# The first rotated queries leave from another buffer, their stores are split by head pair, and the second rope table and stores move in SP's order

## The chip, the core and the metric

The kernel runs on one core of a Trainium2 chip. Its engines are TensorE (PE; its weight loads are shown as PEld), VectorE (DVE), ScalarE (ACT), GpSimd (POOL) and SyncE (SP), which here issues every DMA transfer. Each engine works through its own list of instructions in order, and semaphores tie the lists together. The metric is the device time of one execution in microseconds, lower is better.

## What is computed

One layer on 512 tokens and 16 learned meta tokens (528 positions, width 1024): a norm, one joint projection, two attention branches of 16 heads each (MLA with a rotated part of 32 dimensions, and FoX with a forget gate), and a gated merge. Cut to what matters:

```python
u = rmsnorm(h, pre_norm_g)
(cq, ckv, k_pe_raw, z_mla, fq, fk, fv, f_logit, z_fox, gate_a, gate_b) = split(u @ w_in)
q  = (rmsnorm(cq, g) @ w_uq).reshape(L, 16, 64 + 32)      # q_nope, q_pe
kv = (rmsnorm(ckv, g) @ w_ukv).reshape(L, 16, 64 + 64)    # k_nope, v_mla
q_m = concat(q_nope, rope(q_pe, pos)); k_m = concat(k_nope, rope(k_pe_raw, pos))
o_mla = causal_attention(q_m, k_m, v_mla, scale)
cum   = cumsum(log_sigmoid(f_logit + b))
o_fox = causal_attention(fq, fk, fv, scale, cum)          # logit[t,s] += cum[t] - cum[s]
mixed = (sigmoid(gate_a) * ((o_mla * silu(z_mla)) @ w_a)
       + sigmoid(gate_b) * ((o_fox * silu(z_fox)) @ w_b)) @ w_out
out   = h + rmsnorm(mixed, post_norm_g)
```

## The kernel before

**Numbers in two halves.** Products must be nearly exact, so each operand is kept as a high half and a low half (what rounding left over), and a product is three passes: high by high, high by low, low by high. A weight tile of 128x1024 is loaded by SP (wraw, 512 KB), its high half wh is cast by ACT (L125) and its low half wl is subtracted by POOL (L100). There are three such buffers.

**Stages.** Attention runs in 16 stages, two for each of the eight head pairs: first FoX (even stages, br = 1), then MLA (odd stages, br = 0). So stage 0 is FoX on pair 0, stage 1 is MLA on pair 0, and so on. A stage has these steps:

- score products st into PSUM; DVE takes them out with the mask and the row minimum (sf, nb, L634); ACT takes the exponentials and their sums (L642)
- norm: DVE's reciprocal, then ACT and DVE write the probabilities pn as float16 halves (L669, L670), POOL the piece for the meta tokens (L656 to L661)
- eight DMA transposes by SP turn pn into pt, four blocks of queries for each of two heads. "Turning transfers" below means these.
- values: the products ov of pt and the turned values vp. These wait in the list late and run in the next stage, after its first score products.

Between these PE runs fills, which belong to later stages: projections of queries (fq, mq), keys (fk, mk), values (v), the z gates and the merge gates pg. Each such unit, when it begins, also issues the weight loads of the next three units.

**The rotated queries.** The MLA scores also need the rotated part of the queries for each head. pe_unit(g) makes it for the eight heads of half g: ppe products, DVE's products with a cos and sin table (rope_pe, 512 KB), then rest(x) for x = 0, 1 on POOL: one sum or difference (L518), a cast to the high half (L520), a subtraction for the low half (L100), and two stores to the DRAM tensor qpe_dram (L523). load_qp(pr) later loads one pair back as the tile QP. Half 0 is made before stage 0, half 1 in stages 5 and 6. For half 0 the tables and both halves lie in the room of pt, which is not in use before stage 0's turning transfers; for half 1 they lie in gT, the buffers of the branch outputs.

**What sets the order.** The schedule of PE in the attention is the order of the code. On the other engines a scheduler places instructions by readiness and priority. From the step in_order to the end of stage 0, written[0] is set, and every transfer issued by the helper dma() is then kept in the order of the code on SP's queue. SP takes its list strictly in order: a transfer whose source is not ready holds up all behind it.

**Names in the order lists.** pt_655 and pt_656 are the turned probabilities of the two heads, pn_653 and pn_654 the probabilities, vh and vp_658 / vp_659 the values before and after turning (MLA / FoX), gT_676 and gT_677 the two gT buffers, CT the forget sums of a pair. The wraw numbers of the two builds differ by a few from one point on: 904 before is 943 in the change (weights of fq for pair 1), then 977 (fk) and 993 (v) in both.

Of the kernel before, what the change touches and what calls it, by code (L numbers as in the profile page):

```python
# [49 lines left out]
def f32(ap):  # L50
    return ap.bitcast(F32)
# [3 lines left out]
def block_kernel(ctx: ExitStack, tc: tile.TileContext, x, meta_tokens, pre_norm_g, w_in, fox_forget_b,  # L55
                 mla_q_norm_g, mla_kv_norm_g, w_uq, w_ukv, w_br_mla, w_br_fox, w_out, post_norm_g,
                 rope_tok, rope_pe, out):
    nc = tc.nc
# [20 lines left out]
    c_dram = dram.tile([2, NH, L], F32, tag="cdram", name="c_dram")  # L79
    qpe_dram = dram.tile([NH, 2, 2, 16, S], F32, tag="qpedram", name="qpe_dram")  # L80
# [1 line left out]
    wp = ctx.enter_context(tc.tile_pool(name="wp", bufs=3))  # L82
    uid = [0]
    written = [False]
    behind = []

    def dma(out, src, start=None):

        ins = (start or nc.sync.dma_start)(out=out, in_=src)
        if written[0]:  # L90
            tc.keep_in_program_order(ins)

    def mm(*a, **k):
        nc.tensor.matmul(*a, **k)  # L94
# [4 lines left out]
    def split_lo(eng, lo, src, hi):  # L99
        eng.tensor_tensor(out=lo, in0=src, in1=f32(hi), op=ALU.subtract)  # L100
# [109 lines left out]
    def run(steps):  # L210
        for _, fn in steps:
            fn()
# [6 lines left out]
    CT = fx.tile([128, L], F32R, tag="CT", name="CT")  # L219
# [24 lines left out]
    def k_fox(pr):  # L244
        halves = hl_done(("k", 1, pr), L, HALF)

        def done(i, ps):
            halves(i, ps)
            if pr and i:
                for h in range(2):  # L250
                    ins = nc.sync.dma_start(out=f32(CT[64 * h : 64 * h + 2, :]), in_=c_dram[:, 2 * pr + h, :])
                    if pr == 1:

                        tc.keep_in_program_order(ins)
        return unit(f"fk{pr}", win_w(O_FK, pr), u_act, KD, ALLT, done)


# [167 lines left out]
    with ExitStack() as att:  # L425
# [15 lines left out]
        pn = [ac.tile([128, 2, n, 128], F16, tag=f"pn{g}", name=f"pn{g}") for g, n in enumerate((17, 9))]  # L441

        pts = [ac.tile([128, 9, 512], F16, tag=f"pt{h}", name=f"pt{h}") for h in range(2)]
# [13 lines left out]
        gT = [gpool.tile([128, KD, S], F32, tag=n, name=n) for n in ("gT0", "gT1")]  # L457
# [3 lines left out]
        def load_qp(pr):  # L461
            dma(f32(QP), qpe_dram[2 * pr : 2 * pr + 2].rearrange("h i x f s -> (h i x f) s"))
# [20 lines left out]
        def pe_unit(g):  # L483
            if g == 0:
                r0, tt = (p.rearrange("p a b -> p (a b)")[:, 0 : 8 * S].bitcast(F32).rearrange("p (c s) -> p c s", c=4)
                          for p in pts)
            else:
                r0, tt = gT[0][:, 4:8], gT[1][:, 4:8]
            rp = r0[:, 0:2]

            rr = [r0[:, 2:4], tt[:, 2:4]]
            if g == 0:
                nc.sync.dma_start(rp, rope_pe)
            out = []
            w = {}

            def half(xi, ws=None):
                if ws:
                    w[0] = ws
                return (lambda k: w[0][2 * xi + k][0]), (lambda k: w[0][2 * xi + k][1])  # L500

            def srcs():
                if g:
                    nc.sync.dma_start(rp, rope_pe)
                return [wuqh[:, k, 8 * g : 8 * g + 8, NOPE + 16 * x : NOPE + 16 * x + 16]
                        for x in range(2) for k in range(2)]

            for xi in range(2):
                get = (lambda: half(1)) if xi else weights(srcs, lambda ws: half(0, ws))

                def done(i, ps, xi=xi):
                    for cs in range(2):
                        nc.vector.tensor_tensor(out=tt[:, 2 * xi + cs], in0=ps, in1=rp[:, cs], op=ALU.mult)
                out += unit(f"ppe{g}{xi}", get, cq_act, 2, REAL, done)

            def rest(x):

                nc.gpsimd.tensor_tensor(out=tt[:, x], in0=tt[:, x], in1=tt[:, 3 - x], op=(ALU.subtract, ALU.add)[x])  # L518
                hi, lo = rr[x][:, 0], rr[x][:, 1]
                nc.gpsimd.tensor_copy(hi.bitcast(F32R), tt[:, x])  # L520
                split_lo(nc.gpsimd, lo.bitcast(F32R), tt[:, x], hi)
                for i in range(2):
                    dma(qpe_dram[8 * g : 8 * g + 8, i, x], rr[x][:, i])  # L523
            return out, [[(0, lambda x=x: rest(x))] for x in range(2)]

        mw = {}

# [63 lines left out]
        def attention(br, pr):  # L591
# [54 lines left out]
            def norm(g):  # L646
                def fn():
                    b0, nb_ = GRP[g][0], len(GRP[g])
                    su, ri = (sums[t][:, :, b0 : b0 + nb_] for t in ("su", "ri"))
                    nc.vector.tensor_scalar(out=su, in0=su, scalar1=1.0 / PSCALE, scalar2=None, op0=ALU.mult)  # L650
                    nc.vector.reciprocal(ri, su)  # L651

                    mt = aw.tile([128, 2, nb_, META], F32, tag=f"mt{g}", name=f"mt{nm_}{g}", bufs=1)
                    src = sfs[g][:, :, 0 : SF_STEP * nb_].rearrange("p h (b c) -> p h b c", b=nb_)[:, :, :, 0:META]
                    dst = pn[g][:, :, 0 : PN_STEP * nb_].rearrange("p h (b t) c -> p h b t c", b=nb_)[:, :, :, 0]
                    nc.gpsimd.tensor_tensor(out=mt, in0=src, in1=ri.unsqueeze(3).broadcast_to([128, 2, nb_, META]),  # L656
                                            op=ALU.mult)
                    hi, lo, hi2 = (dst[:, :, :, 32 * i : 32 * i + META] for i in range(3))
                    nc.gpsimd.tensor_copy(hi, mt)
                    nc.gpsimd.tensor_tensor(out=lo, in0=mt, in1=hi, op=ALU.subtract)  # L660
                    nc.gpsimd.tensor_copy(hi2, mt)  # L661
                    for b in GRP[g]:
                        for h in range(2):
                            sf = sf_of(h, b)[:, META:].rearrange("p (j c) -> p j c", c=128)
                            t0 = PN_STEP * (b % 3) + 1
                            hi, lo = (pn[g][:, h, t0 : t0 + 2 * b + 2].rearrange("p (j l) c -> p j l c", l=2)[:, :, i]
                                      for i in range(2))
                            rib = sums["ri"][:, h, b : b + 1]
                            nc.scalar.activation(hi, sf, AF.Copy, scale=rib)  # L669
                            nc.vector.scalar_tensor_tensor(out=lo, in0=sf, scalar=rib, in1=hi, op0=ALU.mult,  # L670
                                                           op1=ALU.subtract)
                    for b in GRP[g]:
                        for h in range(2):
                            t0 = PN_STEP * (b % 3)
                            dma(pts[h][:, 0 : 2 * b + 3, 128 * b : 128 * b + 128],
                                pn[g][:, h, t0 : t0 + 2 * b + 3].rearrange("p t c -> p (t c)"),
                                nc.sync.dma_start_transpose)
                return fn

            def values():  # L680
# [32 lines left out]
                fn.nxt = [f.load for f in fns[n + 1 : n + 4]]  # L713

        v, vts[1, 0] = v_unit(1, 0)
        pe, pe_rest = pe_unit(0)
        g = gate_unit()
        first = pe + v + [(0, in_order)] + vts.pop((1, 0)) + g[:4] + pe_rest[0] + pe_rest[1]
        begun = g[4:]
        fills = []  # L720
        for si, (br, pr) in enumerate(stages):
            last = si + 1 == len(stages)
            if not last:
                q, k, v = feed(*stages[si + 1])
            if br == 1:

                za, zb = z_unit(1, pr), z_unit(0, pr)
                fill = vts.get((br, pr), begun) + za + q + zb[:4] + k + zb[4:6] + v + zb[6:]
            elif not last:

                fill = vts[br, pr] + q + k[:KD] + v + k[KD:]
            else:
                g = gate_unit()
                fill = vts[br, pr] + g + gate_unit() + gate_unit()
            if si == 5:
                pe, pe_rest = pe_unit(1)
                fill[17:17] = pe + pe_rest[0]
            if si == 6:
                fill[17:17] = pe_rest[1]
            fills.append(fill)  # L740
        tail = gate_unit()

# [3 lines left out]
        for si, (br, pr) in enumerate(stages):  # L746
            s0, s1, n0, n1, va = attention(br, pr)

            for fn in [s0] + late + [s1]:
                fn()  # L750

            fill = fills[si]
            run(fill[:5])
            if si == 0:
                load_qp(0)
            n0()
            cut = 12 if si else 5
            run(fill[5:cut])
            n1()
            run(fill[cut:])  # L760
            written[0] = False
            if si == 1:
                behind.clear()
            late = [va]
# [146 lines left out]
```

## Time and profile before

| what | us |
|---|---|
| median of 3 runs (lowest, highest) | 628.37 (627.38, 629.66) |
| the profiled execution | 629.72 |
| its span, first to last instruction | 627.9 |
| mean granted TensorE clock, share of full | 0.994 |
| HBM read and written in the span | 55.21 MB, 4.26 MB |

The span is made up of a front part to about 69 us (norms, first projections), the attention to about 430 us, and the merge and output projection. Engine rows give a start time, a duration, the line, the operation, out<-in tiles, sizes, a count, and in brackets the idle time before it with what ended it. A row of a table by windows gives the stretch, its length, then for PE, PEld, DVE, ACT and POOL the busy time and count, the granted clock, the busy share of the 16 DMA engines and GB/s. A row of SP's queue has the time from the first issue to the end of the last; when the data has landed isn't shown there.

### The profile page before, as it was taken

What the parts mean: (1) busy time and instruction counts of PE and PEld (TensorE: products, weight loads), DVE (VectorE), ACT (ScalarE), POOL (GpSimd) and SP (SyncE); (2) the same over time, 40 slices, a digit from 0 to 9 for tenths busy, and PEclk for the clock granted to TensorE, in tenths of its full rate; (3) what the DMA queues carried; (4) which work ended last, traced back from release to release, by engine and by line L of the source; (5) the groups of instructions that cost most, each with busy time, mean ns of one, the idle gap of its engine ahead of it and who ended that gap; (6) DMA issues with size and microseconds to landing.
All of it is one profiled execution on the core that took longest, in us unless ns stands there. A gap on an engine that the chain in (4) does not pass through costs nothing.

```text
span 627.9 us, 10952 instructions
## 1 busy us (share of the span) xinstructions
PE 604.0 (96%) x3810; PEld 509.4 (81%) x3810; DVE 310.7 (49%) x899; ACT 328.9 (52%) x738; POOL 266.7 (42%) x269
## 2 busy tenths in 40 slices
PE   3999989999999999999999999999999999999996
PEld 2888877888889879789888888887888888888885
DVE  3746753567566665764674666546320122023134
ACT  5657645567665664864684666657322222232321
POOL 3225824434344652443344443541744444444620
PEclk9999997999999999999999999999999999999999
DMA  8441568868788888577579577672433333333702
GB/s 283 107 102 51 120 170 201 194 143 167 156 167 150 188 197 190 120 180 182 132 164 195 137 150 171 167 161 82 135 96 96 89 93 99 100 101 108 262 33 101
DMA packets 223808, 90.10 MB, mean 143 GB/s; under 512 B 141628, under 2 KB 216764, under 8 KB 223752
## 3 DMA queue, kind: packets, MB, share of 16 engines
q1 hardware_dynamic: 223752, 89.39, 59.7%
q8 instruction: 30, 0.49, 0.3%
q14 instruction: 26, 0.21, 0.1%
HBM read 55.21 MB, written 4.26 MB: 95 GB/s over the span
## 4 chain that ended last, share of the span: by engine, by line
PE 74%; DVE 3%; ACT 2%; issue 1%; DMA 0%; SPq 0%; DVEq 0%; ACTq 0%
PE py L94 14%; PE pg L94 13%; PE z L94 12%; PE po L94 7%; PE v L94 7%; PE fk L94 6%; PE fq L94 5%; PE st L94 4%; PE ov L94 3%; DVE sf L634 2%; PE mq L94 2%; ACT wh L125 1%; PE mk L94 1%; DVE vh L570 1%; ACT sil L583 0%
## 5 line engine op out<-in xcount | busy, mean ns | idle before, releaser
L100 POOL TENSOR_TENSOR wl<-wraw,wh 128x1024 fp32r<-128x1024 f32 (+1 forms) x90 | 208.4, 2320 | 224.6 <-ACT wh L125 222.8
L125 ACT CAST wh<-wraw 128x1024 fp32r<-128x1024 f32 (+1 forms) x90 | 89.9, 1001 | 174.8 <-issue 49.9
L642 ACT ACTIVATE sf<-sf,nb 128x144 f32<-128x144 f32 (+3 forms) x128 | 72.0, 564 | 14.9 <-DVE nb L634 14.9
L670 DVE SCALAR_TENSOR_TENSOR pn<-sf,ri,pn 128x128 f16<-128x128 f32 (+3 forms) x128 | 66.0, 554 | 13.2 <-ACT pn L669 12.3
L669 ACT ACTIVATE pn<-sf,ri 128x128 f16<-128x128 f32 (+3 forms) x128 | 61.5, 551 | 19.1 <-ACT sf L642 18.5
L794 DVE SCALAR_TENSOR_TENSOR tb<-th,py 128x512 f32<-128x512 f32 x16 | 11.0, 687 | 101.9 <-PE py L94 101.9
L94 PE MATMUL st<-hlk,hlq 64*128 64x272 f32 (+3 forms) x480 | 52.7, 318 | 1.7 <-ACT hlk L237 0.8
L94 PE MATMUL z<-uTh,wh 128*128 128x512 f32 x128 | 50.9, 398 | 0.0
L94 PE MATMUL pg<-uTh,wh 128*128 128x512 f32 x128 | 50.2, 392 | 0.0
L94 PE MATMUL z<-uTh,wl 128*128 128x512 f32 x128 | 50.0, 391 | 0.0
L94 PE MATMUL z<-uTl,wh 128*128 128x512 f32 x128 | 49.9, 390 | 0.0
L94 PE MATMUL pg<-uTl,wh 128*128 128x512 f32 x128 | 49.9, 389 | 0.0
L94 PE MATMUL pg<-uTh,wl 128*128 128x512 f32 x128 | 49.8, 389 | 0.0
L94 PE MATMUL py<-gh,wh 128*128 128x512 f32 x128 | 49.8, 389 | 0.0
L94 PE MATMUL py<-gl,wh 128*128 128x512 f32 x128 | 49.8, 389 | 0.0
L94 PE MATMUL py<-gh,wl 128*128 128x512 f32 x128 | 49.8, 389 | 0.0
L634 DVE CUSTOM_DVE_ANT_0 sf<-st,maskt 128x272 f32<-128x272 f32 (+2 forms) x128 | 48.3, 433 | 0.8 <-PE st L94 0.8
L94 PEld LDWEIGHTS st<-hlk,hlq 64*128 64x128 f32 x480 | 37.2, 189 | 11.7 <-ACT hlk L237 2.6
L656 POOL TENSOR_TENSOR mt<-sf,ri 128x96 f32<-128x96 f32 (+1 forms) x32 | 9.5, 295 | 87.3 <-DVE ri L651 66.4
L94 PE MATMUL ov<-pt,vp 128*64 128x512 f16 (+4 forms) x416 | 35.2, 318 | 4.3 <-DMA pt<-pn 4.3
L94 PEld LDWEIGHTS <-vp 128*64 128x64 f16 (+1 forms) x416 | 23.3, 113 | 18.0 <-issue 9.5
L94 PE MATMUL v<-uTh,wh 128*128 128x256 f32 (+1 forms) x128 | 36.6, 286 | 0.7 <-DVE hlq L100 0.7
(183 smaller groups left out, 1422.2 us busy)
## 6 DMA issues: line engine op xcount, KB each, us to landing
wraw<-in_w_in_dram SPq DMA_DIRECT2D x56, 512.0 KB
wraw<-in_w_br_fox_dram SPq DMA_DIRECT2D x8, 512.0 KB
wraw<-in_w_br_mla_dram SPq DMA_DIRECT2D x8, 512.0 KB
wraw<-in_w_out_dram SPq DMA_DIRECT2D x8, 512.0 KB
QP<-qpe_dram SPq DMA_DIRECT2D x8, 256.0 KB
pt<-pn SPq DMA_TRANSPOSE x128
xr<-in_x_dram SPq DMA_DIRECT2D x4, 512.0 KB
out_dram<-yo SPq DMA_DIRECT2D x8, 256.0 KB
```

What stands on the lines that cost most here:

```text
L94: nc.tensor.matmul(*a, **k)
L100: eng.tensor_tensor(out=lo, in0=src, in1=f32(hi), op=ALU.subtract)
L125: nc.scalar.copy(wh[:, :n], raw[:, :n])
L570: nc.vector.scalar_tensor_tensor(out=lo, in0=p, scalar=sc[:, 3:4], in1=hi, op0=ALU.mult, op1=ALU.subtract)
L634: nc.vector.tensor_tensor_reduce(out=sf_of(h, b)[:, c0 : c0 + w], in0=ps[h][:, o : o + w], in1=maskt[:, m0 : m0 + w], scale=-scale, scalar ...
L642: nc.scalar.activation(sf, sf, AF.Exp, bias=sums["nb"][:, h, b : b + 1], scale=-1.0, accum_out=sums["su"][:, h, b : b + 1])
L656: nc.gpsimd.tensor_tensor(out=mt, in0=src, in1=ri.unsqueeze(3).broadcast_to([128, 2, nb_, META]), op=ALU.mult)
L669: nc.scalar.activation(hi, sf, AF.Copy, scale=rib)
L670: nc.vector.scalar_tensor_tensor(out=lo, in0=sf, scalar=rib, in1=hi, op0=ALU.mult, op1=ALU.subtract)
L794: nc.vector.scalar_tensor_tensor(out=tb[br], in0=ths[i, br], scalar=1.0, in1=py, op0=ALU.add, op1=ALU.mult)
```

## The change

It has five parts:

- In pe_unit(0) the high and low halves are written to gT[0][:, 4:6] and gT[1][:, 4:6] instead of the room of pt. The table and the unrounded sums stay in pt.
- The stores of half 0 are split by head: in rest(x), two heads (pair 0) of each; the other six heads are stored in stage 1, after that stage's vp transfer.
- The table load of half 1 is kept in the order of the code.
- POOL's rest of half 1 with its stores is written after the second norm of stages 6 and 7, kept in order.
- In stage 0 the fill is cut at 4 instead of 5 steps, and both norms come right behind the load of QP; the loads of CT for pair 1 are placed after the last turning transfer of stage 0.

```diff
-            rr = [r0[:, 2:4], tt[:, 2:4]]
+            rr = [r0[:, 2:4], tt[:, 2:4]] if g else [t[:, 4:6] for t in gT]
...
                 if g:
-                    nc.sync.dma_start(rp, rope_pe)
+
+                    tc.keep_in_program_order(nc.sync.dma_start(rp, rope_pe))
...
                 split_lo(nc.gpsimd, lo.bitcast(F32R), tt[:, x], hi)
+                if g:
+                    store(x, 0, 8)
+                else:
+
+                    store(x, 0, 2)
+
+            def store(x, a, b):
                 for i in range(2):
-                    dma(qpe_dram[8 * g : 8 * g + 8, i, x], rr[x][:, i])
-            return out, [[(0, lambda x=x: rest(x))] for x in range(2)]
+                    dma(qpe_dram[8 * g + a : 8 * g + b, i, x], rr[x][16 * a : 16 * b, i])
+            return out, rest, store
...
             if si == 5:
-                pe, pe_rest = pe_unit(1)
-                fill[17:17] = pe + pe_rest[0]
-            if si == 6:
-                fill[17:17] = pe_rest[1]
+                pe, rest1, _ = pe_unit(1)
+                fill[17:17] = pe
...
-            run(fill[:5])
             if si == 0:
+
+                run(fill[:4])
                 load_qp(0)
-            n0()
-            cut = 12 if si else 5
-            run(fill[5:cut])
-            n1()
-            run(fill[cut:])
+                n0()
+                n1()
+                first_t.extend(through)
+                run(fill[4:])
+            else:
+                run(fill[:1])
+                if si == 1:
+
+                    written[0] = True
+                    for x in range(2):
+                        store0(x, 2, 8)
+                    written[0] = False
+                run(fill[1:5])
+                n0()
+                run(fill[5:12])
+                n1()
+                if 6 <= si < 8:
+
+                    written[0] = True
+                    rest1(si - 6)
+                    written[0] = False
+                run(fill[12:])
```

On PE, ACT and DVE the built lists are the same instructions in the same order. SP's list differs at three places, POOL's at one.

SP ahead of stage 0's turning transfers, before:

```order
L504 DMA gT_676<-in_rope_pe_dram 128x1024
L89 DMA_TRANSPOSE vp_659<-vh 128x9x128
L89 DMA wraw_790<-in_w_in_dram 128x8x128
L89 DMA qpe_dram<-pt_655 8x16x512 x2
L89 DMA qpe_dram<-pt_656 8x16x512 x2
L89 DMA wraw_904<-in_w_in_dram 128x8x128
L89 DMA QP<-qpe_dram 128x512
L89 DMA_TRANSPOSE pt_655<-pn_653 128x3x128
```

The same place in the change:

```order
L89 DMA_TRANSPOSE vp_659<-vh 128x9x128
L89 DMA wraw_790<-in_w_in_dram 128x8x128
L89 DMA qpe_dram<-gT_676 2x16x512 x2
L89 DMA qpe_dram<-gT_677 2x16x512 x2
L89 DMA QP<-qpe_dram 128x512
L89 DMA_TRANSPOSE pt_655<-pn_653 128x3x128
```

The second table has gone from the head (it is now in stage 3), the stores have 2 heads instead of 8, and the weight load 904 is no longer ahead of the QP load.

SP from the last turning transfer of stage 0 to the first of stage 1, before:

```order
L89 DMA_TRANSPOSE pt_656<-pn_654 128x9x128
L89 DMA wraw_977<-in_w_in_dram 128x8x128
L89 DMA wraw_993<-in_w_in_dram 128x8x128
L89 DMA_TRANSPOSE vp_658<-vh 128x9x128
L89 DMA wraw_1172<-in_w_in_dram 128x8x128
L89 DMA wraw_1231<-in_w_uq_dram 128x2x64 x2
L89 DMA wraw_1231<-in_w_ukv_dram 128x2x64 x2
L89 DMA wraw_1281<-in_w_in_dram 128x8x128
L251 DMA CT<-c_dram 2x528
L89 DMA_TRANSPOSE pt_655<-pn_653 128x3x128
```

The same place in the change:

```order
L89 DMA_TRANSPOSE pt_656<-pn_654 128x9x128
L89 DMA wraw_943<-in_w_in_dram 128x8x128
L89 DMA wraw_977<-in_w_in_dram 128x8x128
L89 DMA wraw_993<-in_w_in_dram 128x8x128
L89 DMA CT<-c_dram 2x528 x2
L89 DMA_TRANSPOSE vp_658<-vh 128x9x128
L89 DMA qpe_dram<-gT_676 6x16x512 x2
L89 DMA qpe_dram<-gT_677 6x16x512 x2
L89 DMA wraw_1176<-in_w_in_dram 128x8x128
L89 DMA wraw_1235<-in_w_uq_dram 128x2x64 x2
L89 DMA_TRANSPOSE pt_655<-pn_653 128x3x128
```

Three weight loads instead of two follow stage 0's turning transfers, and the four stores of six heads stand between the vp transfer and stage 1's turning transfers. ACT's list has the casts of all three loads (wh of 943, 977 and 993) ahead of stage 1's first exponential, as before.

SP in stage 6, before:

```order
L89 DMA wraw_2665<-in_w_in_dram 128x8x128
L89 DMA qpe_dram<-gT_676 8x16x512 x2
L89 DMA qpe_dram<-gT_677 8x16x512 x2
L89 DMA wraw_2724<-in_w_in_dram 128x8x128
L89 DMA_TRANSPOSE vp_659<-vh 128x9x128
L89 DMA wraw_2741<-in_w_in_dram 128x8x128
L89 DMA_TRANSPOSE pt_655<-pn_653 128x3x128
```

The same place in the change:

```order
L89 DMA wraw_2664<-in_w_in_dram 128x8x128
L89 DMA wraw_2723<-in_w_in_dram 128x8x128
L89 DMA_TRANSPOSE vp_659<-vh 128x9x128
L89 DMA wraw_2740<-in_w_in_dram 128x8x128
L89 DMA_TRANSPOSE pt_655<-pn_653 128x3x128
```

The four stores of half 1 have left; two now follow the last turning transfer of stage 6, two that of stage 7, where the load of QP for pair 4 stands behind them. On POOL, before stage 0, the low half of mq's weights (wl_974) now stands ahead of the casts and low halves of the rotated queries instead of behind them.

More of the change, by code (lines that the diff above doesn't have):

```diff
@@ L84, in block_kernel @@
     written = [False]
-    behind = []
+    behind, through, first_t = [], [], []
     def dma(out, src, start=None):
@@ L91, in dma @@
             tc.keep_in_program_order(ins)
+        return ins.ins
     def mm(*a, **k):
@@ L250, in done @@
                 for h in range(2):
-                    ins = nc.sync.dma_start(out=f32(CT[64 * h : 64 * h + 2, :]), in_=c_dram[:, 2 * pr + h, :])
-                    if pr == 1:
-                        tc.keep_in_program_order(ins)
+                    with tc.issue_after(first_t[0]) if pr == 1 else nullcontext():
+                        dma(f32(CT[64 * h : 64 * h + 2, :]), c_dram[:, 2 * pr + h, :])
         return unit(f"fk{pr}", win_w(O_FK, pr), u_act, KD, ALLT, done)
@@ L674, in fn @@
                             t0 = PN_STEP * (b % 3)
-                            dma(pts[h][:, 0 : 2 * b + 3, 128 * b : 128 * b + 128],
-                                pn[g][:, h, t0 : t0 + 2 * b + 3].rearrange("p t c -> p (t c)"),
-                                nc.sync.dma_start_transpose)
+                            through[:] = [dma(pts[h][:, 0 : 2 * b + 3, 128 * b : 128 * b + 128],
+                                              pn[g][:, h, t0 : t0 + 2 * b + 3].rearrange("p t c -> p (t c)"),
+                                              nc.sync.dma_start_transpose)]
                 return fn
@@ L715, in block_kernel @@
         v, vts[1, 0] = v_unit(1, 0)
-        pe, pe_rest = pe_unit(0)
+        pe, rest0, store0 = pe_unit(0)
+        pe_rest = [(0, lambda x=x: rest0(x)) for x in range(2)]
         g = gate_unit()
-        first = pe + v + [(0, in_order)] + vts.pop((1, 0)) + g[:4] + pe_rest[0] + pe_rest[1]
+        first = pe + v + [(0, in_order)] + vts.pop((1, 0)) + g[:4] + pe_rest
         begun = g[4:]
```

## The prediction

> **What bounds the kernel now.** I read the page's first part, then TensorE's own waits, then its timeline at the two places that the waits point to.
>
> ```profile
> PE 604.0 (96%) x3810; PEld 509.4 (81%) x3810; DVE 310.7 (49%) x899; ACT 328.9 (52%) x738; POOL 266.7 (42%) x269
> ```
>
> Of a span of 627.9 us, TensorE (PE) is busy for 604.0. So a change that adds no product can win only what PE waits, and what it loses to a slower clock. The waits, as total, times and longest:
>
> ```profile
> PE pt L97 <- DVE hn L337: 7.9, 2, 7.3
> PE ov L94 <- DMA pt<-pn: 4.3, 4, 2.1
> ```
>
> The 7.9 us lie at the start, where nothing changes. The second row is the one that the change is near: the value products ov wait for turned probabilities pt. Its places (start, duration, wait before it in brackets):
>
> ```profile
> 90.12 0.56 PE L94 MATMUL st<-hlk,hlq 64*128 64x144 f32 x6
> 92.13 0.35 PE L94 MATMUL st<-KPL,QP 64*128 64x400 f32 x2
> 94.59 0.45 PE L94 MATMUL ov<-pt,vp 80*64 80x512 f16 x1 [2.11 <-DMA pt<-pn]
> 95.94 3.79 PE L94 MATMUL ov<-pt,vp 80*64 80x512 f16 x25 [0.91 <-DMA pt<-pn]
> 101.93 0.50 PE L94 MATMUL fq<-uTh,wh 128*128 128x512 f32 x1
> 114.28 0.39 PE L94 MATMUL v<-uTh,wh 128*128 128x256 f32 x1 [0.68 <-DVE hlq L100]
> ...
> 182.74 0.56 PE L94 MATMUL st<-hlk,hlq 64*128 64x144 f32 x6
> 188.46 0.50 PE L94 MATMUL fq<-uTh,wh 128*128 128x512 f32 x1
> ...
> 228.10 0.56 PE L94 MATMUL st<-hlk,hlq 64*128 64x144 f32 x6
> 231.33 0.38 PE L94 MATMUL ov<-pt,vp 80*64 80x512 f16 x1 [0.86 <-DMA pt<-pn]
> 232.11 2.01 PE L94 MATMUL ov<-pt,vp 80*64 80x512 f16 x25 [0.41 <-DMA pt<-pn]
> 235.46 0.50 PE L94 MATMUL fq<-uTh,wh 128*128 128x512 f32 x1
> ```
>
> Stage 5 has no wait: from its first score product to its first fq product it needs 188.46 - 182.74 = 5.72 us. The same work takes 11.81 us in stage 1 (loss 6.09) and 7.36 us in stage 7 (loss 1.64). Stage 1 waits only 3.02 us. The other 3.07 us are the clock, the last but two of these columns:
>
> ```profile
> 96.00:98.00 2.00, 2.00 (x12) 1.17 (x13) 0.00 (x0) 0.00 (x0) 0.00 (x0) 0.50 0.94 255
> 102.00:104.00 2.00, 2.00 (x10) 1.66 (x10) 0.00 (x0) 2.00 (x9) 2.00 (x2) 1.00 0.52 151
> 230.00:234.00 4.00, 2.73 (x32) 1.77 (x28) 3.38 (x16) 3.00 (x13) 2.79 (x3) 1.00 0.99 229
> ```
>
> The long wait of stage 1 halves it; the two short ones of stage 7 (1.27 us together) do not. With the 0.68 us at the v product, at most 6.09 + 0.68 + 1.64 = 8.4 us can be won.
>
> Why the turned probabilities are late, on SP's queue (a start, and the time until the row's last issue is through):
>
> ```profile
> 73.27 3.89 SPq L89 DMA_DIRECT2D qpe_dram<-pt  x4
> 77.20 1.50 SPq L89 DMA_DIRECT2D wraw<-in_w_in_dram  x1
> 83.22 0.35 SPq L89 DMA_DIRECT2D QP<-qpe_dram  x1
> 83.68 10.63 SPq L89 DMA_TRANSPOSE pt<-pn  x8
> 94.78 1.01 SPq L89 DMA_DIRECT2D wraw<-in_w_in_dram  x2
> ...
> 206.77 4.33 SPq L89 DMA_DIRECT2D qpe_dram<-gT  x4
> 212.54 5.34 SPq L89 DMA_TRANSPOSE vp<-vh  x1
> 218.68 1.35 SPq L89 DMA_TRANSPOSE pt<-pn  x1
> ```
>
> In stage 0 SP stands from 78.70 to 83.22 at the QP load, which needs the four stores landed; all eight turning transfers are behind it. In stage 6 four stores of the second half clog the queue: the vp transfer behind them takes 5.34 us.
>
> **The change, part by part.** *Stage 6.* The four stores leave that place; two follow the turning transfers of stage 6, two those of stage 7. The vp transfer and the pt transfers then go out when their sources are ready, and stage 7 loses its wait: 1.64 us won. If another thing still holds SP there, nothing is won. The second rope table moves from ahead of stage 0's vp transfer into stage 3's turning transfers. I cost it at nothing, since the list has no wait for pt but those of stages 1 and 7, so stage 3's have room; with the room gone it would cost at most its 512 KB at the 343 GB/s shown below, 1.5 us.
>
> *Stage 0, the small stores.* The first halves lie in gT, so the room of pt is free as soon as POOL has read it. But SP's order keeps the QP load, with its wait, ahead of the turning transfers. All depends on when four stores of 64 KB, in place of four of 256 KB, have landed. What POOL does last ahead of them, and how the large ones flow (last two columns: busy share of the 16 DMA engines, GB/s):
>
> ```profile
> 71.59 1.27 POOL L100 TENSOR_TENSOR pt<-pt,pt 128x512 fp32r<-128x512 f32 x1
> 72.83 1.28 POOL L100 TENSOR_TENSOR wl<-wraw,wh 128x512 fp32r<-128x512 f32 x1
> ...
> 76.00:79.50 3.50, 3.50 (x17) 2.89 (x16) 2.93 (x7) 3.50 (x8) 0.99 (x4) 1.00 0.53 185
> 97.50:98.50 1.00, 1.00 (x9) 0.77 (x7) 0.00 (x0) 0.00 (x0) 0.00 (x0) 0.50 1.15 343
> ```
>
> A weight load, in the last row, fills all engines (343 GB/s). From 76.0 on the stores run alone, and only 0.53 of the engines are busy, 8.5 of 16, at 185 / 8.5 = 21.8 GB/s each. The store has 8 heads in its outer dimension, so I read this as one engine for each head. Then a store of two heads has two engines: each carries 4 x 32 KB = 131 KB, 6.0 us, exactly as each of the eight does now. Splitting by pair cuts the bytes by four and the engines by four. What does leave is the weight load at 77.20, which now shares those engines: half of its 512 KB on eight engines is 262 / 185 = 1.4 us. The QP load thus goes out at 83.22 - 1.4 = 81.8. Bounds: no later than now, 83.22; and if the small stores were spread over all 16, POOL's last half, done at 72.86 now, is done at about 74.1 (the weight split of 1.28 us goes ahead of it), issue 0.6, 262 KB at 343 GB/s 0.8, landing 1.6 as for the last turning transfer (94.31 to 95.94): 77.1.
>
> That is what the Trainium skill says too ("DMA: Bandwidth & Descriptors", section "Why a DMA increments its semaphore by 16 and not by 1"): the engines of one DMA are the largest number up to 16 that divides the outer sizes of both sides. It speaks against this split; by it 8 and 2 engines serve the two shapes, and the 0.53 in the row agrees for the first.
>
> *Stage 1, what is late next.* Call E the end of the eighth turning transfer's issue: QP issue + 0.46 + 10.63, now 94.31, by my value 92.9 (88.2 to 94.3). Behind it there are now three weight loads, not two: the one at 77.20 (fq's) has moved there. Their landings, and what ACT does after them:
>
> ```profile
> 99.31 1.05 ACT L125 CAST wh<-wraw 128x1024 fp32r<-128x1024 f32 x1 [6.74 <-DMA wraw<-in_w_in_dram]
> 100.81 1.05 ACT L125 CAST wh<-wraw 128x1024 fp32r<-128x1024 f32 x1 [0.46 <-DMA wraw<-in_w_in_dram]
> 101.76 0.41 ACT L642 ACTIVATE sf<-sf,nb 128x144 f32<-128x144 f32 x1
> 112.93 0.57 ACT L237 CAST hlq<-fq 128x512 fp32r<-128x512 f32 x1
> ...
> 92.65 2.35 POOL L100 TENSOR_TENSOR wl<-wraw,wh 128x1024 fp32r<-128x1024 f32 x1 [2.45 <-ACT wh L125]
> ```
>
> The first lands at E + 5.0, each further one 1.5 later; ACT, in order, starts stage 1's exponentials only after the last cast, E + 7.45 now and E + 8.95 with three. From there to the v product that PE waits for are 114.28 - 101.76 = 12.5 us, fixed work of ACT and DVE. So as long as PE gets to v before ACT is through, stage 1 wins 101.76 - (E + 8.95) = 92.8 - E, however much of the wait for pt has gone: -0.1 us at my E, +4.6 and -1.5 at the bounds. PE does get there first: fq's low half is ready at E + 5.0 + 1.05 + 2.4 = E + 8.45 (a new wait of some 2.5 us at fq), and v is 11.7 us behind fq.
>
> *Behind that.* Four stores of six heads (six engines, again 131 KB each) go ahead of stage 1's turning transfers. The same load in stage 6 cost PE 1.64 us a stage later: bounds 0 and 1.64, I take 0.2, since here stage 2 itself starts late.
>
> Sum: 1.64 - 0.1 - 0.2 = 1.3 us: the span goes from 627.9 to 626.6. That execution took 629.72 us in all; the runs' median is 628.37, so I forecast 627.0 us.
>
> **Rivals.** *The small stores land at once* (engines do not follow the heads): QP at 77.1, E = 88.2, no wait for pt, a short one at v: 4.6 + 1.64 = 6.2, 622.1 us. For it: only a shape of eight heads was seen. Against it: the 0.53.
>
> *Slower: the weights behind the turning transfers.* With E at 94.3, stage 1 loses 1.5, and PE stands for pt (some 2.5 us), then at fq (2.5). If the clock halves there too, that costs 3.07, of which the wait at v hides 1.8. With 1.64 won in stage 6: 628.4 + 1.5 + 1.3 - 1.6 = 629.6 us, and 631.2 if stage 2 then waits the full 1.64 behind the six-head stores. It decides once the turning transfers start after about 83 and fq waits over 2 us. For it: a halved clock followed 3 us of waiting; against it: 1.27 us did nothing.
>
> The Trainium skill ("TensorE: Matmul & The Clock Gate", section "Part 1: The HAM clock gate") halves the clock after an idle window of about 3.4 us; by that rule waits of 2.5 us with work between would leave it alone, and 628.3 would remain of this case.
>
> *No gain in stage 6* (vp or a load still holds SP): 628.4 + 0.3, about 628.7, no change.
>
> **How the numbers follow.** The forecast has 0.52, quick stores 0.22, the slower case 0.13, no gain in stage 6 0.13. About 0.3%, 1.9 us, can be told from no change, so faster begins at 626.5. The forecast's own range is 625.3 to 628.6: 0.22 of its 0.52 below 626.5, 0.28 within, 0.02 above 630.3. With the quick stores, faster is 0.44; slower gets 0.08 of the slower case and 0.02 of the last, 0.12 in all; the same keeps 0.44. The range that leaves out at most 2 in 10 is 621.8 to 630.0.
>
> **What would show it.** Right: the QP load near 81.8, DMA share near 0.13 while the small stores run, exponentials of stage 1 near 101.8, PE with a new wait at fq and a longer one at v, and none for pt in stage 7. Wrong: turning transfers from 78 on (quick stores); exponentials before 99 or after 103.5; a clock of 0.50 past 102; a wait for pt in stage 2 or 7.

## The result, and the profile after

The changed kernel takes 628.00 us in the median of 20 runs (626.57 to 630.23). The kernel before, run beside it, takes 629.17 in 20 runs (627.38 to 632.06). The ratio is 0.9984, with a 95% interval of 0.9973 to 0.9996: about 1.0 us less, between 0.3 and 1.7. The forecast was 627.0, that is 1.4 us less. The profiled execution took 628.52 us, with a span of 626.7.

TensorE's waits after the change, from the list of waits (total, times, longest):

```profile
PE pt L98 <- DVE hn L337: 7.6, 1, 7.6
PE v L95 <- DVE hlq L101: 3.0, 1, 3.0
...
PE fq L95 <- POOL wl L101: 1.7, 1, 1.7
...
PE ov L95 <- DMA pt<-pn: 0.8, 1, 0.8
```

The wait for pt has gone from 4.3 us to 0.8. Two waits have come in its place: 1.7 us at fq and 3.0 at v, where there was 0.7. TensorE's timeline in stages 1 and 7 (start, duration, wait before it):

```profile
88.87 0.56 PE L95 MATMUL st<-hlk,hlq 64*128 64x144 f32 x6
92.35 2.01 PE L95 MATMUL ov<-pt,vp 80*64 80x512 f16 x25 [0.78 <-DMA pt<-pn]
95.94 0.50 PE L95 MATMUL fq<-uTh,wh 128*128 128x512 f32 x1 [0.16 <-ACT wh L126]
98.37 0.50 PE L95 MATMUL fq<-uTh,wl 128*128 128x512 f32 x1 [1.69 <-POOL wl L101]
112.57 0.39 PE L95 MATMUL v<-uTh,wh 128*128 128x256 f32 x1 [2.99 <-DVE hlq L101]
120.00 0.56 PE L95 MATMUL st<-hlk,hlq 64*128 64x144 f32 x6
...
227.86 0.56 PE L95 MATMUL st<-hlk,hlq 64*128 64x144 f32 x6
230.16 2.04 PE L95 MATMUL ov<-pt,vp 80*64 80x512 f16 x26
232.12 0.72 PE L95 MATMUL st<-hlk,hlq 64*128 64x272 f32 x6
232.86 0.96 PE L95 MATMUL st<-hlk,hlq 64*128 64x256 f32 x6
233.98 0.50 PE L95 MATMUL fq<-uTh,wh 128*128 128x512 f32 x1
```

In the kernel before, stage 2's first score product stands here:

```profile
120.23 0.56 PE L94 MATMUL st<-hlk,hlq 64*128 64x144 f32 x6
```

Read the stages by their lengths, because the two executions don't start alike: at stage 1's first score product the changed kernel is 1.25 us ahead (88.87 against 90.12). That lead is no work of the change. It is there, 1.24 us, at a group of weight loads 63 us earlier, long before the first transfer that the change moves (the second table's load, at 67.84 in the kernel before). SP's queue, before and after:

```profile
26.89 2.68 SPq L89 DMA_DIRECT2D wraw<-in_w_uq_dram  x4
67.84 0.36 SPq L504 DMA_DIRECT2D gT<-in_rope_pe_dram  x1
```

```profile
25.65 2.59 SPq L89 DMA_DIRECT2D wraw<-in_w_uq_dram  x4
```

From stage 1's first score product to stage 2's, the kernel before needs 120.23 - 90.12 = 30.11 us, the changed one 31.13. Stage 1 is won at the value products and lost again behind them, and a little more. Stage 7, from its first score product to fq, goes from 7.36 to 6.12 us.

How stage 1 lost it again is in the clock. The windows below are (length, then busy time and instructions of PE, PEld, DVE, ACT and POOL, then the granted clock, the DMA share and GB/s):

```profile
74.50:79.00 4.50, 4.50 (x21) 3.72 (x21) 3.94 (x9) 4.50 (x10) 1.18 (x5) 1.00 0.14 52
96.48:99.89 3.41, 1.72 (x8) 1.26 (x8) 0.00 (x0) 1.94 (x2) 2.99 (x2) 1.00 1.12 181
110.13:113.54 3.41, 0.97 (x8) 0.98 (x9) 2.46 (x5) 1.94 (x4) 2.15 (x1) 1.00 1.11 163
113.55:116.95 3.40, 3.40 (x18) 3.40 (x18) 0.00 (x0) 0.00 (x0) 0.21 (x1) 0.50 1.36 190
116.96:120.37 3.41, 3.41 (x32) 3.28 (x33) 2.12 (x8) 2.01 (x5) 1.47 (x2) 1.00 1.01 224
```

Behind the 2.99 us at v the clock is half for 3.41 us, and nothing that PE waits for comes later in the stage, so the lost products are lost time: from the v product to stage 2 PE needs 120.00 - 112.57 = 7.43 us, in the kernel before 120.23 - 114.28 = 5.95. In the kernel before, the clock halved in the value products, for 6.83 us, where ACT was late anyway.

SP's queue shows what the small stores did:

```profile
71.51 2.70 SPq L89 DMA_DIRECT2D qpe_dram<-gT  x4
79.55 0.36 SPq L89 DMA_DIRECT2D QP<-qpe_dram  x1
80.01 10.59 SPq L89 DMA_TRANSPOSE pt<-pn  x8
91.06 1.98 SPq L89 DMA_DIRECT2D wraw<-in_w_in_dram  x3
```

The QP load waits until 79.55, that is 8.04 us after the first small store's start; in the kernel before it was 83.22 - 73.27 = 9.95. A quarter of the bytes needs four fifths of the time. While these stores run alone, the DMA share is 0.14 (first row of the windows), which is 2.2 engines of 16.

### The profile page after: what moved, and what is told of

Its sections match the earlier page's. It is cut to its first block, busy times and chain, and to the rows that moved or that the text cites. A ratio compares the mean times of both kernels' runs of the same rounds, so it can differ in the third digit from the quotient of the medians.

```text
span 626.7 us, 10961 instructions
## 1 busy us (share of the span) xinstructions
PE 602.4 (96%) x3810; PEld 507.7 (81%) x3810; DVE 310.4 (50%) x899; ACT 329.0 (52%) x738; POOL 266.5 (43%) x269
## 4 chain that ended last, share of the span: by engine, by line
PE 86%; DVE 4%; ACT 3%; issue 2%; DMA 2%; SPq 1%; POOL 0%; DVEq 0%; ACTq 0%
PE pg L95 14%; PE py L95 14%; PE z L95 14%; PE v L95 9%; PE fk L95 7%; PE po L95 7%; PE fq L95 7%; PE st L95 4%; PE psm L95 3%; PE ov L95 3%; DVE sf L642 2%; ACT wh L126 2%; PE mq L95 2%; PE mk L95 1%; DMA wsr<-in_w_in_dram 1%
## 5 line engine op out<-in xcount | busy, mean ns | idle before, releaser
L650 ACT ACTIVATE sf<-sf,nb 128x144 f32<-128x144 f32 (+3 forms) x128 | 72.0, 564 | 14.9 <-DVE nb L642 14.9
L642 DVE CUSTOM_DVE_ANT_0 sf<-st,maskt 128x272 f32<-128x272 f32 (+2 forms) x128 | 48.3, 433 | 0.8 <-PE st L95 0.8
L95 PE MATMUL v<-uTl,wh 128*128 128x256 f32 (+1 forms) x128 | 37.2, 291 | 0.0
L95 PE MATMUL v<-uTh,wl 128*128 128x256 f32 (+1 forms) x128 | 37.1, 290 | 0.0
```

The source lines that it names most:

```text
L642: nc.vector.tensor_tensor_reduce(out=sf_of(h, b)[:, c0 : c0 + w], in0=ps[h][:, o : o + w], in1=maskt[:, m0 : m0 + w], scale=-scale, scalar ...
L650: nc.scalar.activation(sf, sf, AF.Exp, bias=sums["nb"][:, h, b : b + 1], scale=-1.0, accum_out=sums["su"][:, h, b : b + 1])
```

## The experiments

Ratios are to the kernel before on the same chip, with 95% intervals. The table has one profiled execution for each kernel, in us. Stage 1's first score product is the zero of columns 3 and 4, because the starts differ. "Exponentials" is ACT's first one of stage 1 (L642 in the old code, L650 in the change, L654 in e1, e5 and e6). "To stage 2" runs from stage 1's first score product to stage 2's. The clock column has the times at half clock ahead of the last product.

| kernel | first score product | QP load ahead | exponentials behind | PE waits at pt, fq, v | half clock | to stage 2 | ratio (interval) |
|---|---|---|---|---|---|---|---|
| before | 90.12 | 6.90 | 11.64 | 3.02, 0, 0.68 | 94.76 to 101.59 | 30.11 | 1 |
| the change | 88.87 | 9.32 | 11.08 | 0.78, 1.85, 2.99 | 113.54 to 116.96 | 31.13 | 0.9984 (0.9973 to 0.9996) |
| the change again (e8) | 88.72 | 9.31 | 11.02 | 0.84, 2.86, 1.07 | 98.93 to 102.34 | 30.21 | 0.9995 (0.9979 to 1.0010) |
| stages 0 and 1 alone (e3) | 88.66 | 9.41 | 11.02 | 0.71, 1.95, 2.71 | 112.91 to 116.33 | 30.85 | 0.9997 (0.9986 to 1.0008) |
| stages 6 and 7 alone (e4) | 89.09 | 8.07 | 10.83 | 1.99, 0, 3.50 | 113.38 to 116.79 | 30.65 | 0.9990 (0.9980 to 1.0000) |
| table alone (e7) | 90.42 | 7.43 | 11.58 | 2.64, 0, 2.19 | 95.28 to 98.69, 115.76 to 119.17 | 31.44 | 1.0011 (0.9996 to 1.0025) |
| fq's load ahead (e2) | 90.31 | 8.43 | 10.79 | 1.65, 0, 2.19 | 94.97 to 98.38 | 29.15 | 0.9987 (0.9976 to 0.9997) |
| 16-row stores (e1) | 90.57 | 13.22 | 7.45 | 0, 0, 2.52 | none | 25.81 | 0.9922 (0.9909 to 0.9935) |
| e1 and e2 (e5) | 89.13 | 13.45 | 4.39 | 0, 0, 1.49 | none | 24.78 | 0.9913 (0.9890 to 0.9936) |
| e5, loads moved up (e6) | 89.17 | 13.52 | 4.23 | 1.82, 0, 0 | none | 25.21 | 0.9904 (0.9880 to 0.9927) |

**The shape of the small stores (e1_spread).**

```diff
 def store(x, a, b):
+    if b - a == 2:
+        for h in range(a, b):
+            dma(qpe_dram[8 * g + h, :, x].rearrange("i f s -> f i s"), rr[x][16 * h : 16 * h + 16, :])
+        return
     for i in range(2):
         dma(qpe_dram[8 * g + a : 8 * g + b, i, x], rr[x][16 * a : 16 * b, i])
```

> The changed kernel, but the four small stores are cut the other way: one store for each head and x, of 16 rows with both parts i side by side, in place of one for each i and x with two heads outside. As many stores, the same bytes, the same place in SP's order. My theory (the number of DMA engines follows the outer dimension, two before, 16 now): the small stores have landed by about 76 to 77 us, the QP load goes 2.5 to 3.5 us earlier than the 79.55 of the changed kernel (both counted from a stage 0 that starts alike), the eight turning transfers and the exponentials of stage 1 with it (99.95 becomes about 96.5), no wait for pt in stage 1, the wait at v falls from 2.99 to about 1.2 and with it goes the halved clock of 113.5 to 116.9: 3.8 + 1.46, about 5 us less, 623 us in the median. Rival (the stores' time is a fixed landing time or their bytes, not their shape): QP load unchanged at about 79.5, 628 us.

Measured: 624.67 us in the median, ratio 0.9922. SP's queue, and a window in which the small stores run:

```profile
73.30 2.02 SPq L89 DMA_DIRECT2D qpe_dram<-gT  x4
77.35 0.34 SPq L89 DMA_DIRECT2D QP<-qpe_dram  x1
```

```profile
76.00:76.50 0.50, 0.50 (x4) 0.40 (x3) 0.47 (x3) 0.50 (x3) 0.40 (x2) 1.00 0.96 345
```

TensorE, at v and at stage 2:

```profile
110.43 0.39 PE L95 MATMUL v<-uTh,wh 128*128 128x256 f32 x1 [2.52 <-DVE hlq L101]
116.38 0.56 PE L95 MATMUL st<-hlk,hlq 64*128 64x144 f32 x6
```

As many bytes in as many stores are through 4.05 us after the first one's start, not 8.04: all engines are busy (0.96, 345 GB/s) where two were before (0.14, 52 GB/s). The wait for pt is gone and the clock stays full. The expected 5 us are there in stage 1 of these two profiles (31.13 to 25.81); in the medians the step from the change to e1 is 0.9984 to 0.9922, about 3.9 us. The rival falls. The remaining wait at v was expected at 1.2 and is 2.5: ACT's third weight cast came only at 97.06, 8.2 us after the loads were issued.

**The order of fq's load (e2_early).** Five steps of the fill, not four, ahead of the QP load:

```diff
-                run(fill[:4])
+                run(fill[:5])
                 load_qp(0)
...
-                run(fill[4:])
+                run(fill[5:])
```

> The changed kernel, but fq's weight load stands ahead of the QP load again, as before the change; nothing else moves on SP. My theory (three loads behind the turning transfers make ACT late at the exponentials of stage 1, so PE waits 1.69 us at fq and 2.99 at v, and the second wait halves the clock): the load shares the two engines of the small stores, so the QP load goes up to 1.75 us later; the wait at fq goes, the wait for pt in stage 1 grows from 0.78 to between 1.5 and 2.5, the wait at v falls below 1.5 and the clock stays full there: 0 to 2 us less than the changed kernel, 626.5 in the median, the more the less the clock falls in the ov products instead. Rival (the order of that load doesn't matter, the turning transfers alone set it): stage 1 as in the changed kernel, 628.

Measured: 628.26 us, ratio 0.9987: no different from the change. The waits moved as expected at fq (gone) and pt (1.65 in all), but v still waits 2.19, and the clock halves in the value products:

```profile
91.56:94.97 3.41, 1.76 (x19) 1.11 (x17) 3.35 (x16) 1.20 (x2) 2.12 (x1) 1.00 0.88 186
94.98:98.38 3.40, 3.40 (x27) 2.47 (x25) 0.00 (x0) 1.05 (x1) 0.23 (x2) 0.50 1.20 324
```

The load runs beside the two-engine stores and makes the QP load 0.9 us later, which eats most of what one load fewer behind the turning transfers wins: the exponentials come at 10.79, not 11.08. With slow stores the order of this load is worth nothing that shows in the medians, though stage 1 is shorter in this one profile (29.15).

**The two parts alone (e3_half0, e4_half1).** e3 puts the second half's rest back into the fills of stages 5 and 6 and lets the scheduler place the second table again; e4 is the kernel before with these lines changed, and two more that only hand the function rest out of pe_unit:

```diff
-                    nc.sync.dma_start(rp, rope_pe)
+                    tc.keep_in_program_order(nc.sync.dma_start(rp, rope_pe))
...
-                pe, pe_rest = pe_unit(1)
-                fill[17:17] = pe + pe_rest[0]
-            if si == 6:
-                fill[17:17] = pe_rest[1]
+                pe, _, rest1 = pe_unit(1)
+                fill[17:17] = pe
...
             n1()
+            if 6 <= si < 8:
+                written[0] = True
+                rest1(si - 6)
+                written[0] = False
             run(fill[cut:])
```

> The changed kernel with its part at stages 0 and 1 alone: the second half's stores and rope table go back to where they stood before. My theory: this part wins the waits of the value products and gives them back at fq and v, so that it is worth between nothing and 1.0 us of loss; with the 1.27 us of waiting back in stage 7: 629.2 to 630.2 us in the median, slower than the changed kernel by about 1.2. Rival (the gain of the change comes from stage 1, that of the profile's start being chance): 628, and stage 7 without its wait.

> The kernel before with the change's other part alone: the second half's stores behind the turning transfers of stages 6 and 7, and its rope table inside those of stage 3. Stages 0 and 1 stay as before. My theory: stage 7 loses its two waits (1.27 us, 1.2 to 1.6 in all), stage 1 keeps its 3.02 us of waiting for pt and its halved clock: 627.8 us in the median, as fast as the whole change or up to 1 us faster. Rival (the stage 6 part gains nothing by itself): 629.2.

Measured: e3 629.48 us, ratio 0.9997; e4 628.64 us, ratio 0.9990; the kernel before 629.54 beside them. So the part at stages 0 and 1 is worth nothing that shows, and e4, between its theory (627.8) and its rival (629.2), has about what the change wins. The medians alone don't settle this, since the two intervals overlap (e3 0.9986 to 1.0008, e4 0.9980 to 1.0000). Stage 7 does. In e3 the value products wait for pt there again, in e4 they don't:

```profile
230.74 2.04 PE L95 MATMUL ov<-pt,vp 80*64 80x512 f16 x25 [0.65 <-DMA pt<-pn]
```

```profile
230.12 2.04 PE L94 MATMUL ov<-pt,vp 80*64 80x512 f16 x26
```

From its first score product to fq, stage 7 takes 6.11 to 6.13 us in all seven profiles with the moved stores, and 7.36, 7.26 and 6.72 in the three without (before, e7, e3).

One thing in e4 was not expected. Its stage 1 has the old stores and the old order, and yet the clock halves behind v, as in the change, and not in the value products. Its two waits for pt fell into two different windows of 3.41 us, with 2.35 and 2.48 us of work each; the wait at v was 3.50:

```profile
92.41 0.38 PE L94 MATMUL ov<-pt,vp 80*64 80x512 f16 x1 [0.96 <-DMA pt<-pn]
93.81 2.01 PE L94 MATMUL ov<-pt,vp 80*64 80x512 f16 x25 [1.03 <-DMA pt<-pn]
112.32 0.39 PE L94 MATMUL v<-uTh,wh 128*128 128x256 f32 x1 [3.50 <-DVE hlq L100]
```

**The second table alone (e7_table).** After e4 it looked as if the table's move made stage 0's stores earlier. The kernel before, with the first two changed lines of e4's diff and nothing else:

> The kernel before, and of the change only the move of the second rope table from ahead of stage 0's vp transfer into the turning transfers of stage 3. My theory after the first four runs: the 512 KB no longer run beside that vp transfer and the weight load behind it, so the four stores and the QP load go about 1.1 us earlier (8.1 us ahead of stage 1's first score product in place of 6.9); the exponentials of stage 1 come 10.8 us after that product in place of 11.6. What that wins is taken or left by the clock at v, so 628.5 to 629.5 us, stage 7 with its two waits as before. Rival (my costing at nothing holds): the QP load stays 6.9 us ahead, 629.5.

Measured: 630.28 us, ratio 1.0011, no change. The QP load is 7.43 ahead, half of what was expected, and the exponentials are at 11.58, as before the change (11.64). My theory falls: up to stage 5 e4 has the same code as e7, so most of its lead was its own execution's. The costing at nothing stands.

**The change once more (e8_after_again).** The same kernel, unchanged.

> The changed kernel once more, for a second profile and a ratio on this chip. My theory: the 1.24 us by which its first profile was ahead at the first score product of stage 1 is the luck of one execution (the starts of six profiles lie between 88.66 and 90.57), and what repeats is the exponentials 11.0 to 11.2 us behind that product, a wait for wl at fq of 1.7, one of 2.5 to 3 at v, and none for pt in stage 7. Whether the clock halves behind v may differ from one execution to the next. 0.9984 of the time before, within its interval (0.9973 to 0.9996). Rival (the early start belongs to the change): ahead by over 1 us again.

Measured: 629.20 us beside 629.45, ratio 0.9995 (0.9979 to 1.0010); the two intervals of the change overlap from 0.9979 to 0.9996, and the second one does not exclude that nothing is won. The start is early again, but the ten profiles settle that it belongs to the execution: stage 1's first score product starts between 88.66 and 90.57, yet in all ten it comes 63.19 to 63.24 us behind the group of weight loads shown above (x4), so the differences arise in the first 27 us, which no edit touches. The exponentials repeat to 0.06 us. The clock does not: here it halves at fq, where v hides it, and stage 1 is 0.9 us shorter than in the first profile. From v to stage 2 it needs 118.93 - 112.99 = 5.94 us, not 7.43.

```profile
96.83 0.50 PE L95 MATMUL fq<-uTh,wh 128*128 128x512 f32 x1 [1.15 <-ACT wh L126]
99.27 0.79 PE L95 MATMUL fq<-uTh,wl 128*128 128x512 f32 x1 [1.71 <-POOL wl L101]
112.99 0.39 PE L95 MATMUL v<-uTh,wh 128*128 128x256 f32 x1 [1.07 <-DVE hlq L101]
```

```profile
95.52:98.92 3.40, 0.89 (x6) 0.30 (x2) 0.00 (x0) 2.22 (x3) 2.06 (x1) 1.00 1.21 240
98.94:102.33 3.39, 3.06 (x7) 2.48 (x8) 0.00 (x0) 3.39 (x12) 3.39 (x3) 0.50 0.45 113
```

**Quick stores and the load ahead (e5_both).** The two diffs of e1 and e2 together.

> The two edits of e1 and e2 together: small stores over 16 rows, and fq's load ahead of the QP load. Times counted from the first score product of stage 1, since the starts of the runs differ. My theory (exponentials of stage 1 wait for ACT's last weight cast, v resumes 12.4 to 12.6 us behind them): the QP load goes 0.5 to 1.75 us later than in e1, the turning transfers too, but two loads stand behind them and not three, so the exponentials come 6.5 to 7.2 us after the first score product (7.45 in e1) and the wait at v falls from 2.52 to about 1.9: 0.3 to 0.9 us less than e1, 624 us. Rival (the third load costs nothing where the stores are quick): as e1, 624.7.

Measured: 624.11 us, ratio 0.9913. The QP load goes no later than in e1 (13.45 ahead, 13.22 there): where all engines serve the stores, the load beside them costs nothing. The exponentials come at 4.39, not 6.5 to 7.2, right behind three casts that run back to back, so ACT no longer waits for a load. But v does not follow them by 12.4 to 12.6 us, as in seven of the profiles (13.25 in e8): 107.98 - 93.52 = 14.46. ACT waits for DVE, and DVE for POOL:

```profile
90.52 3.09 ACT L126 CAST wh<-wraw 128x1024 fp32r<-128x1024 f32 x3
99.13 2.51 ACT L681 ACTIVATE pn<-sf,ri 128x128 f16<-128x128 f32 x6 [2.47 <-DVE ri L663]
```

```profile
96.69 2.12 DVE L662 TENSOR_SCALAR su<-su 128x6 f32<-128x6 f32 x1 [2.96 <-ACT sf L654]
98.85 0.19 DVE L663 RECIPROCAL ri<-su 128x6 f32<-128x6 f32 x1
```

```profile
91.67 7.12 POOL L101 TENSOR_TENSOR wl<-wraw,wh 128x1024 fp32r<-128x1024 f32 x3 [2.45 <-ACT wh L126]
```

DVE's sum of 128x6, 0.17 us in e1, takes 2.12 here and ends at 98.81, as POOL's last subtraction does (91.67 + 7.12 = 98.79). All ten profiles fit: where the sum starts behind POOL's subtraction it takes 0.17 us (five profiles), and where it starts before that ends, it ends 0.03 us or less behind it (0.28 in the kernel before, 0.39 in the change, 1.02 in e8, 2.12 here, 2.20 in e6). The 1.02 is also why v came 13.25 us behind the exponentials in e8. The Trainium skill ("SBUF — State Buffer", section "SBUF: two separate sides") says that GpSimd and some VectorE operations, by their mode or their number of inputs, share one pair of ports, which the one that starts first keeps for its whole instruction. These rows agree; the profile doesn't show the mode of this sum, and no run here tried it by itself.

**The loads between the turning transfers (e6_mid).** e5, with the fill up to the sixteenth step between the two norms of stage 0:

```diff
                 load_qp(0)
                 n0()
+                run(fill[5:16])
                 n1()
                 first_t.extend(through)
-                run(fill[5:])
+                run(fill[16:])
```

> e5, and the two weight loads that stood behind the eight turning transfers of stage 0 now stand between the sixth and the seventh of them. My theory: they land 2.7 us earlier, the last cast and the exponentials of stage 1 with them (4.0 to 4.5 us after the first score product), v is ready before PE comes to it, and PE waits nowhere in stages 1 to 15; the last two turning transfers go about 1 us later and are still in time (they land about 1.5 us after the first score product, the value products start 2.3 after it). 2.2 to 2.6 us less than e1: 622.2 us. Rival (ACT, not the loads, is what makes the exponentials late, its casts only fill its time): the wait at v stays near 2, 624.

Measured: 623.24 us, ratio 0.9904, not to be told from e5 (0.9913). The rival was right on the mechanism: the exponentials come at 4.23, as in e5, since ACT's casts were not waiting for the loads any more. The last two turning transfers, behind the loads, took 4.50 us and were not in time:

```profile
85.66 4.50 SPq L89 DMA_TRANSPOSE pt<-pn  x2
```

```profile
93.69 2.01 PE L95 MATMUL ov<-pt,vp 80*64 80x512 f16 x25 [1.82 <-DMA pt<-pn]
```

The 1.82 us at pt have taken the place of the 1.49 at v. e5 and e6 are both faster than the kernel before and the changed kernel, by about 5.5 to 6 us against the former.

## Why the prediction was right, and where it was not

**The stores: right.** Splitting by pair took engines away with the bytes: a DMA share of 0.14 while they run, 0.13 forecast, and e1, with the same bytes on all engines, got the QP load 3.9 us earlier (13.22 ahead, 9.32 in the change). The QP load was put at 81.8 on the old clock, 8.32 us ahead of stage 1; it is 9.32 ahead. So E was 1.0 us earlier than forecast, in both profiles of the change. No run takes this 1.0 apart. The first small store starts 0.5 us earlier against stage 1 (17.36 ahead of it, 16.85 before), and 52 GB/s on the 2.2 engines of the share are 23 each, where the forecast, reckoned in the same way, had 21.8; by that rate, an estimate, 131 KB take about 5.6 us and not 6.0.

**Three loads behind the turning transfers: right.** The exponentials were to come at E + 8.95; with E at 90.60 that is 99.55, and they came at 99.95. The wait at fq was put at some 2.5 us and measures 1.85 and 2.86. What e5 adds: with the stores quick, the third load is worth 3.1 us of the exponentials (7.45 to 4.39), not 1.5.

**Stage 1's gain of -0.1: right in size, wrong in its working.** The step said: as long as PE gets to v before ACT is through, stage 1 wins 92.8 - E. That sets when v starts: 24.16 us behind the first score product before, 23.70 after, a gain of 0.46. The step failed behind it: I priced a halved clock at pt and fq, where the wait at v hides it, and none at v, where nothing does. It cost 31.13 - 30.11 + 0.46 = 1.48 us in the first profile, and was listed among what would prove me wrong (a clock of 0.50 past 102). The profiles repeat it: from the v product to stage 2 PE needs 7.42 to 7.45 us in the four where the clock halves there (the change, e3, e4, e7) and 5.93 to 5.95 in the five where it waits at v and keeps its clock. It is not the change's alone. Over three profiles each, stage 1 with the old stores lasts 30.11, 30.65 and 31.44 us, with the split ones 31.13, 30.21 and 30.85; both means are 30.73. That fits e3's 0.9997, though three profiles that differ by over 1 us are few for a mean.

**Stage 6: right, the term too large.** The 1.64 us came from stage 5, whose score products follow the value products without a stop. In stage 7 the last twelve take 0.72 and 0.96 us, where the kernel before needs 0.65 and 0.52. DVE, which must empty the score buffers, begins with stage 7's scores 3.0 us behind the first score product, in stage 5 2.6; that this stretches the products fits, and no run tests it. So 7.36 - 6.12 = 1.24 us were won against the first profile, 0.6 against e3's 6.72, and e4's 0.9990 is 0.6 us, up to 1.3. The 0.2 us for the six-head stores did not show: neither profile of the change has a wait for pt in stage 2 (only e5 has one, of 0.64).

**How much of the number was luck.** The forecast for the span was 1.3 us less, and the two profiles differ by 1.2. But this 1.2 is a start 1.25 us earlier, which is chance, 1.02 lost in stage 1 and 1.24 won in stage 7, with 0.3 lost behind it. The profiles agree with the sum by luck. In the medians the starts even out, and there 1.0 us is left (0.25 in the second set of runs, e8), of which the experiments put about all in stage 7.

**The rivals.** The quick stores did not come by themselves, but e1 shows most of their price: 6.2 us less was forecast for them, 629.54 - 624.67 = 4.9 measured, and the wait at v that was to be short is 2.52. The slower case had its mechanism in part: the weights are late and the clock then halves, at v in one profile of the change, where it costs 1.5 us, and at fq in the other, where v hides it. The old kernel's stage 1 halves its clock as often (before, e4, e7).

**The clock rule.** The prediction read the Trainium skill ("TensorE: Matmul & The Clock Gate", section "Part 1: The HAM clock gate") as leaving waits of 2.5 us alone. The window of about 3.4 us that runs freely, as the Trainium skill has it there, agrees with the traces: the half clock lasts 3.41 us, or twice that. That the window has to be idle does not: PE was busy for 0.97 us of the one before 113.54, and in e2 for 1.76 of the one before 94.98. The measurement decides.

## What to carry to other kernels

Before a transfer is made smaller to be quicker, look at how its shape spreads over the DMA engines: here a quarter of the bytes on a quarter of the engines still took four fifths of the time, and the same bytes laid over 16 rows made the kernel 4 us faster. Where one engine's chain sets the time of a stage, removing an earlier wait only moves the waiting to the next point, and the new place may cost more if a slow clock follows it with nothing left to hide it. And compare stages by their lengths, not by their times: a start that differs by 1.9 us from one execution to the next is more than this whole change.

## What the runs showed of the hardware

The half clock comes on a grid. In each profile its starts lie at whole multiples of 3.413 us behind the clock's first rise (19.67 in the kernel before, 17.97 in the change, where the products of 128x432 go from 0.56 to 0.36 us): 22 of them in the kernel before and in e2, 28 in the change, e3 and e4, 22 and 28 in e7, 24 in e8. Whether it falls goes with how long PE was busy in the 3.41 us ahead. With 0.83 to 1.34 us busy the clock fell each of seven times; with 1.86 or more it never did in ten profiles. In between the order isn't clean: it fell at 1.76 in e2, and not at 1.72 in the change (second row of its windows) or 1.69 in e3, so the busy time of the profile is not the whole rule. At half clock, 2.50 us of work kept it down for a second window (before, 94.76 to 98.17), and 2.88 in e7 brought it back. So a wait of 2.52 us left the clock full where it lay across two windows (e1: 1.86 us busy in the worse one), and two waits of 1.65 us together in one window halved it (e2). Where the grid falls differs from one execution to the next, so the same kernel lost 1.5 us behind v in one profile and nothing in the other.
